# Attention in a two-layer decoder step: block transposes on VectorE and value products in 4 x 2 tiles

## The chip, the cores and the metric

One Trainium2 chip, one of its cores. The metric is the device time of one execution in microseconds; lower is better. The program is one launch that does two layers for 512 prompt tokens and 8 sample tokens together.

## The reference, cut to what matters

Each layer has one wide input projection, a depthwise conv branch, a sliding-window attention branch, two gates and an output projection. All arithmetic is in fp32.

```
h = rms_norm(x, norm_g)
glu, gate_a, q, k, v, gate_b, mg_a, mg_b = split(h @ w_in)
u = glu_a * sigmoid(glu_b)
c = conv31(u) + conv_b
c = silu(layer_norm(c)) * silu(gate_a)
y_a = c @ w_conv_out
o = attend(rope(q), rope(k), v, sinks)     # 16 heads of 64, 2 kv heads
y_b = (o * silu(gate_b)) @ w_attn_out
y = sigmoid(mg_a) * y_a + sigmoid(mg_b) * y_b
x = x + y @ w_out
```

The prompt's attention runs in 4 blocks of 128 queries. A block sees the 128 keys of the block before and its own 128, of these only the last 128 positions for each query, and one sink per head in the softmax's denominator:

```
s = (q @ k^T) / 8, masked to 0 <= diff < 128
m = max(max(s), sink);  p = exp(s - m)
o = (p / (sum(p) + exp(sink - m))) @ v
```

## The kernel before, in words

Activations lie with channels on the 128 partitions and 520 tokens (512 and 8) along the free dimension. A `Unit` is one 128-column slice of the weights against all 1024 input channels: its weights come in one DMA (`raw`), ScalarE rounds them to fp32r (`whi`, L109), VectorE takes the remainder (`wlo`, L110), and TensorE adds up, for each of 8 k-tiles and each half of 260 tokens, three products: hi x hi, lo x hi, hi x lo (L124). A half is 24 products, a unit 48. Two pairs of PSUM banks (`mmp`) hold units; four banks are left: two for scores and small sums (`psS`), one for transposed probabilities (`psT`), one for value products (`psV`).

The order of a layer: 16 units for the glu, then K, V, eight for Q (`W_Q`), eight for `gate_b` (`W_GB`, with Silu on the way out of PSUM, into `sgb`), then the attention loop, with eight units each of `W_MB` and `W_MA` (the merge gates) as filling between its steps, then eight of `W_GA`, eight of `W_YB` (on the attention's output `oh`/`ol`), eight of `W_YA` (on the conv's output `ch`/`cl`) and eight of `W_OUT`.

The attention loop has 32 steps, pairs (t, b) of a head pair t (one head of each kv head) and a block b. A step's `scores` makes the logits on TensorE (L474), masks them and takes the minimum on VectorE (L480), exponentiates and sums on ScalarE (L486) and scales the probabilities by the reciprocal (L489 to L491). Three steps later (`LAG`) `transposes` turns them on TensorE (L500) and ScalarE copies them to SBUF (L502). When the four blocks of t are turned, `values` multiplies them by v on TensorE (L509): the two kv heads write the lower and the upper 64 partitions of one bank. VectorE multiplies by the gate (L514, L517) and `split` rounds into `oh` and `ol` (L96, L97).

The conv is 31 taps per channel tile on VectorE: a multiply-add of 512 columns each, 240 a layer with the last ones (L563). They are traced with `tc.cur_priority` raised by 2000, so they are the work that VectorE does when nothing else is ready. Behind the last tap come the sums of the layer norm (L155, L160), mean (L574), subtraction (L577), squares (L187), `rstd`, scaling (L581), Silu (L602), the product with `sga` (L604) and the split into `ch` and `cl` (L96, L97), which `W_YA` needs.

A planner places the instructions at build time by priority and by its own prices; each engine then runs its list strictly in that order and waits on semaphores. DMAs for weights and q are issued from SP's queue, the small ones and those for the sample tokens from POOL's. A tile of a pool is given out again when its last reader is done.

Of the kernel before, what the change touches and what calls it, by code (L numbers as in the profile page):

```python
# [16 lines left out]
T = 512  # L17
NS = 8
TOK = T + NS
# [24 lines left out]
def hybrid_step(ctx, tc, x_in, w_in, par, const, rope, conv_st, kc_in, vc_in,  # L44
# [6 lines left out]
    gp = ctx.enter_context(tc.tile_pool(name="gp", bufs=42))  # L51
# [19 lines left out]
    def og(dt=F32):  # L71
        return gp.tile([128, TOK], dt, tag="o", bufs=16, name=name("o"))
# [21 lines left out]
    def split(src, n=TOK, new=g):  # L94
        hi, lo = new(F32R), new(F32R)
        A.copy(hi[:, :n], src)  # L96
        mark[0] = V.tensor_tensor(lo[:, :n], src, hi[:, :n].bitcast(F32), op=ALU.subtract)  # L97
        return hi, lo

    class Unit:  # L100


        def __init__(self, l, idx, hs, los, spare=False):
            self.hs, self.los = hs, los
            raw = wp.tile([128, KT, 128], F32, tag="raw", bufs=2, name=name("raw"))
            nc.sync.dma_start(raw, w_in[l, idx].rearrange("p (k c) -> p k c", k=KT))
            self.hi = wp.tile([128, KT, 128], F32R, tag="whi", name=name("whi"))
            self.lo = wp.tile([128, KT, 128], F32R, tag="wlo", name=name("wlo"))
            A.copy(self.hi, raw)  # L109
            V.tensor_tensor(self.lo, raw, self.hi.bitcast(F32), op=ALU.subtract)  # L110
            if spare:
                banks = [psT.tile([128, 512], F32, tag="T", name=name("T")),
                         psV.tile([128, 512], F32, tag="V", name=name("V"))]
                self.acc = [b[:, :HALF] for b in banks]
# [53 lines left out]
    def rstd(sums, halves=(0, 1)):  # L168
        y0, v, a = tmp("y0", 1), tmp("v", 1), tmp("a", 1)
# [53 lines left out]
    for l in range(L):  # L223
# [138 lines left out]
        A.copy(vb[:, :512], vtp)  # L362
        vsp = sbank()
# [37 lines left out]
        qs = {}  # L401

        def load_q(t):
            for kv in range(2):
                q = g(F32R)
                nc.sync.dma_start(q[:, :T].bitcast(F32), qscr[2 * t + kv])
                qs[t, kv] = q

        sgb = []
        for t in range(8):  # L410
            ps = Unit(l, W_GB + t, hh, hl).both()
            s = g()
            A.activation(two(s), ps, AF.Silu)  # L413
            sgb.append(s)
            if t == 3:
                load_q(0)
# [27 lines left out]
        def sample_transpose():  # L444
            pst = psT.tile([128, 512], F32, tag="T", name=name("pst"))
# [5 lines left out]
        def sample_values():  # L451
            pvs = psV.tile([128, 512], F32, tag="V", name=name("pvs"))
# [8 lines left out]
        oh, ol, mgb, mga = [], [], [], []  # L461
        pts, probs = {}, {}
        exp_ins = [None]

        def scores(t, b):
            if b == 0:
                if t < 7:
                    load_q(t + 1)
                pts[t] = ap.tile([128, 2, 7, 128], F32, tag="pts", bufs=1, name=name("pts"))
            k0, nk = (0, 128) if b == 0 else ((b - 1) * 128, 256)  # L470
            S3 = sbank().rearrange("p (v k) -> p v k", v=2)
            for kv in range(2):
                for j, K in enumerate((KH, KL)):
                    PE.matmul(S3[:, kv, :], qs[t, kv][:, b * 128:b * 128 + 128],  # L474
# [17 lines left out]
            probs[t, b] = p  # L492

        def transposes(t, b):
            p = probs.pop((t, b))
            PT = psT.tile([128, 2, 2, 128], F32, tag="T", name=name("PT"))
            nb = 1 if b == 0 else 2
            for kv in range(2):
                for kb in range(nb):
                    PE.transpose(PT[:, kv, kb, :], p[:, kv, kb * 128:kb * 128 + 128], ident)  # L500
            j0 = 2 * b + 1 - nb
            A.copy(pts[t][:, :, j0:j0 + nb, :], PT[:, :, :nb, :])  # L502

        def values(t):
            pv = psV.tile([128, 512], F32, tag="V", name=name("pv"))
            for j in (0, 2, 1, 3):
                nb = 2 if j < 3 else 1
                for kv in range(2):
                    PE.matmul(pv[kv * 64:kv * 64 + 64, j * 128:(j + nb) * 128],  # L509
                              vb[:, j * 128 + kv * 64:j * 128 + kv * 64 + 64],  # L510
                              pts[t][:, kv, 2 * j:2 * j + nb, :].rearrange("p a b -> p (a b)"),
                              start=(j == 0), stop=(j == 3))
            o = tmp("sq", 3)
            V.tensor_tensor(o[:, :T], pv, sgb[t][:, :T], op=ALU.mult)  # L514
            for kv in range(2):
                r = slice(kv * 64, kv * 64 + 64)
                V.tensor_tensor(o[r, T:], smp["o"][r, :, 2 * t + kv], sgb[t][r, T:], op=ALU.mult)  # L517
            a, b = split(o, new=og)
            oh.append(a)
            ol.append(b)  # L520

        LAG = 3
        order = [(t, b) for t in range(8) for b in range(4)]
        cur = None
        for n in range(len(order) + LAG + 1):
            if n < len(order):
                scores(*order[n])
                if n == 0:
                    sample_scores()
                if n % 2 == 0:  # L530
                    cur = Unit(l, (W_MB, W_MA)[n // 2 % 2] + n // 4, hh, hl)
                cur.half(n % 2)
                if n % 2 == 1:
                    m = g()
                    A.copy(two(m), cur.ps)
                    (mgb, mga)[n // 2 % 2].append(m)
# [4 lines left out]
            if n > LAG and order[n - LAG - 1][1] == 3:  # L541
                values(order[n - LAG - 1][0])
            if LAG <= n < len(order) + LAG:
                transposes(*order[n - LAG])
# [67 lines left out]
        yh, yl = [], []  # L612
        for i in range(KT):
# [3 lines left out]
            a, b = split(mga[i], new=og)  # L617
# [39 lines left out]
        def scale(hf):  # L657
            return rstd([sq.total(hf)], (hf,))
# [132 lines left out]
```

## Time and profile before

| | |
|---|---|
| Time, median of 3 runs | 1074.85 us (1074.48 to 1075.6) |
| The profiled execution's own time | 1074.0 us |
| Its span, first to last instruction | 1072.2 us |
| Mean granted TensorE clock | 0.997 |
| TensorE busy | 1053.9 us, 98% |
| VectorE busy | 854.2 us, 80% |
| ScalarE busy | 514.0 us, 48% |
| GpSimd busy | 79.3 us, 7% |
| Instructions | 21484 |

Busy time is the union of an engine's instructions; matmuls overlap in the array, so a busy TensorE isn't TensorE at its peak, and a matmul's duration is longer than the distance to the next. PE is TensorE, PEld its weight loads, DVE VectorE, ACT ScalarE, POOL GpSimd, SP the queue that issues most DMAs. A row names its line in the kernel, the tile written and the tiles read, without numbers.

### The profile page before, as it was taken

How to read it: one execution, taken by the hardware profiler on the slowest of the kernel's cores; microseconds unless marked ns; L12 is line 12 of the kernel's file. 1: busy time of each engine (PE TensorE's matmuls, PEld its weight loads, DVE VectorE, ACT ScalarE, POOL GpSimd, SP SyncE). 2: the span in 40 equal slices, each digit the busy share in tenths (PEclk: the TensorE clock that was granted, in tenths of full speed). 3: DMA queues.
4: the chain of work that ended last, by engine and by line, in shares of the span. 5: the costliest groups of instructions: out<-in, count | busy, mean ns of one | idle time of the engine just before them, and what ended most of it. 6: DMA issues, size and time to landing. Idle time of an engine off the chain costs nothing.

```text
span 1072.2 us, 21484 instructions
## 1 busy us (share of the span) xinstructions
PE 1053.9 (98%) x8724; PEld 1032.2 (96%) x8724; DVE 854.2 (80%) x1568; ACT 514.0 (48%) x949; POOL 79.3 (7%) x185
## 2 busy tenths in 40 slices
PE   7999999999999999999999999999999999999996
PEld 7999999999999999999999999999999999999995
DVE  5999999999999587455569999999999976944545
ACT  6622443356666785224453234334666686822321
POOL 1011221000001100000101013100000000000000
PEclk9999999999999999999999999999999999999998
DMA  5443574332222225223334337633232313252312
GB/s 218 130 129 111 168 253 149 101 117 80 99 82 72 68 70 189 95 99 113 134 99 139 119 119 247 201 103 119 80 116 67 95 41 99 86 175 96 98 60 80
DMA packets 44115, 126.41 MB, mean 118 GB/s; under 512 B 6176, under 2 KB 8816, under 8 KB 44016
## 3 DMA queue, kind: packets, MB, share of 16 engines
q1 hardware_dynamic: 37440, 110.23, 31.3%
q0 software_dynamic: 5136, 13.45, 3.9%
q8 instruction: 68, 1.11, 0.4%
q10 hardware_dynamic: 1440, 1.37, 0.4%
q14 instruction: 31, 0.25, 0.1%
HBM read 107.66 MB, written 17.36 MB: 117 GB/s over the span
## 4 chain that ended last, share of the span: by engine, by line
PE 95%; DVE 3%; DMA 1%; ACT 0%; issue 0%; SPq 0%; DVEq 0%; ACTq 0%
PE mm L124 85%; PE S L474 3%; PE pv L509 3%; PE PT L500 2%; DMA raw<-w 1%; PE T L124 1%; DVE g L663 1%; DVE wlo L110 1%; DVE sq L235 1%; PE S L160 0%; DVE g L97 0%; PE S L432 0%; PE pvs L454 0%; PE V L124 0%; ACT whi L109 0%
## 5 line engine op out<-in xcount | busy, mean ns | idle before, releaser
L124 PE MATMUL mm<-g,whi 128*128 128x260 f32 x4160 | 771.3, 284 | 7.6 <-ACT g L202 7.0
L124 PEld LDWEIGHTS mm<-g,whi 128*128 128x128 f32 x4160 | 646.3, 188 | 14.4 <-ACT g L202 7.4
L124 PE MATMUL mm<-g,wlo 128*128 128x260 f32 x2080 | 589.2, 284 | 0.0
L124 PEld LDWEIGHTS mm<-g,wlo 128*128 128x128 f32 x2080 | 393.1, 189 | 1.0 <-issue 0.8
L563 DVE SCALAR_TENSOR_TENSOR acc<-u,par,acc 128x512 f32<-128x512 f32 x464 | 329.6, 746 | 0.2
L109 ACT CAST whi<-raw 128x1024 fp32r<-128x1024 f32 x164 | 172.2, 1050 | 206.7 <-PE mm L124 167.3
L110 DVE TENSOR_TENSOR wlo<-raw,whi 128x1024 fp32r<-128x1024 f32 x164 | 200.4, 1223 | 55.3 <-ACT whi L109 55.1
L124 PE MATMUL mm<-o,whi 128*128 128x260 f32 x992 | 178.9, 282 | 0.4 <-DVE g L652 0.4
L124 PEld LDWEIGHTS mm<-o,whi 128*128 128x128 f32 x992 | 153.0, 188 | 0.6 <-DVE g L652 0.6
L124 PE MATMUL mm<-o,wlo 128*128 128x260 f32 x496 | 139.5, 282 | 0.0
L124 PEld LDWEIGHTS mm<-o,wlo 128*128 128x128 f32 x496 | 93.2, 188 | 0.0
L486 ACT ACTIVATE p<-p,sm 128x257 f32<-128x257 f32 (+1 forms) x128 | 60.9, 478 | 12.4 <-DVE sm L480 12.3
L502 ACT COPY pts<-PT 128x256 f32<-128x256 f32 (+1 forms) x64 | 33.8, 528 | 62.1 <-PE PT L500 61.9
L480 DVE CUSTOM_DVE_ANT_0 p<-S,con,nsk 128x256 f32<-128x256 f32 (+1 forms) x128 | 52.6, 448 | 10.9 <-PE PT L500 9.3
L478 POOL COPY p<-nsk 128x2 f32<-128x2 f32 x64 | 23.4, 369 | 360.8 <-PE PT L500 284.3
L615 DVE TENSOR_TENSOR g<-mm,g 128x520 f32<-128x520 f32 x16 | 11.2, 700 | 42.9 <-PE mm L124 42.9
L474 PE MATMUL S<-g,g 128*128 128x256 f32 x256 | 42.1, 284 | 0.0
L609 DVE TENSOR_TENSOR g<-mm,g 128x520 f32<-128x520 f32 x16 | 11.2, 699 | 32.0 <-PE mm L124 32.0
L413 ACT ACTIVATE g<-mm 128x520 f32<-128x520 f32 x16 | 9.7, 607 | 55.9 <-PE mm L124 55.9
L500 PE MATMUL PT<-con,p 128*128 128x128 f32 x224 | 35.6, 276 | 0.0
L474 PEld LDWEIGHTS S<-g,g 128*128 128x128 f32 x256 | 35.2, 189 | 0.4 <-DVE sm L480 0.4
L490 ACT ACTIVATE p<-p,sm 128x128 f32<-128x128 f32 (+1 forms) x64 | 29.8, 479 | 6.4 <-DVE sm L489 6.4
(167 smaller groups left out, 817.0 us busy)
## 6 DMA issues: line engine op xcount, KB each, us to landing
raw<-w SPq DMA_DIRECT2D x164, 512.0 KB, 3.4
qscr<-g SPq DMA_DIRECT2D x32, 256.0 KB, 4.5
g<-qscr SPq DMA_DIRECT2D x32, 256.0 KB, 3.7
g<-x SPq DMA_DIRECT2D x16, 260.0 KB, 7.2
g<-rope POOLq DMA_DIRECT2D x8, 260.0 KB, 4.0
xres<-g POOLq DMA_DIRECT2D x8, 260.0 KB, 2.3
g<-xres SPq DMA_DIRECT2D x8, 260.0 KB, 4.3
g<-conv_state POOLq DMA_DIRECT2D x8, 248.0 KB, 3.4
```

What stands on the lines that cost most here:

```text
L109: A.copy(self.hi, raw)
L110: V.tensor_tensor(self.lo, raw, self.hi.bitcast(F32), op=ALU.subtract)
L124: PE.matmul(self.acc[hf], a[:, k, :], b[k][:, c], start=(k == 0 and j == 0), stop=(k == KT - 1 and j == 2))
L474: PE.matmul(S3[:, kv, :], qs[t, kv][:, b * 128:b * 128 + 128], K[kv][:, k0:k0 + 256], start=(j == 0), stop=(j == 1))
L478: G.tensor_copy(p[:, :, nk:nk + 1], nsk[:, 2 * t:2 * t + 2].unsqueeze(2))
L480: V.tensor_tensor_reduce(out=p[:, kv, :nk], in0=S3[:, kv, :nk], in1=con[:, C_MASK + 256 - nk:C_MASK + 256], op0=ALU.add, op1=ALU.min, scal ...
L486: exp_ins[0] = A.activation(p[:, kv, :nk + 1], p[:, kv, :nk + 1], AF.Exp, bias=nm[:, kv:kv + 1], scale=-1.0, accum_out=dn[:, kv:kv + 1])
L490: A.mul(p[:, 0, :nk], p[:, 0, :nk], dn[:, 0:1])
L500: PE.transpose(PT[:, kv, kb, :], p[:, kv, kb * 128:kb * 128 + 128], ident)
L502: A.copy(pts[t][:, :, j0:j0 + nb, :], PT[:, :, :nb, :])
L509: PE.matmul(pv[kv * 64:kv * 64 + 64, j * 128:(j + nb) * 128], vb[:, j * 128 + kv * 64:j * 128 + kv * 64 + 64], pts[t][:, kv, 2 * j:2 * j + ...
L563: V.scalar_tensor_tensor(dst, us[i][:, k:k + T], cw(i, k), acc[i], op0=ALU.mult, op1=ALU.add)
```

## The change

The attention's steps are ordered by groups n of four head pairs and one block, (tg, b), with four steps t4 in each. The probabilities of a step are no longer transposed on TensorE through PSUM: VectorE transposes each 32 x 32 block in place of its own into `pts[n]`. Keys in those blocks stand rotated over the four groups of 32 partitions, so the values are kept in four copies, three of them rotated by 32, 64 and 96 partitions through DMAs from POOL's queue (`vr`). The value products have 32 rows and 64 columns each: for query group a and diagonal d, one product for each kv head, 128 columns wide (four head pairs of 32 queries), five diagonals added up in PSUM; the four query groups have a bank each. ScalarE copies the four banks, VectorE multiplies by the gates, and both split into wider tiles `oh` and `ol` of four head pairs. The separate pools `psT` and `psV` are gone; `psS` has four banks, for scores, values and all else. q is loaded for four heads and one block per DMA, rows of 512 bytes.

The units are reordered: four `W_GB` units stay ahead of the loop and four go into it, as its first filling, with their Silu after step 8; eight `W_MB` and four `W_MA` follow as filling, and four `W_MA` come behind the loop.

```diff
-    gp = ctx.enter_context(tc.tile_pool(name="gp", bufs=42))
+    gp = ctx.enter_context(tc.tile_pool(name="gp", bufs=41))
-    psS = ctx.enter_context(tc.tile_pool(name="psS", bufs=2, space=bass.MemoryType.PSUM))
-    psT = ctx.enter_context(tc.tile_pool(name="psT", bufs=1, space=bass.MemoryType.PSUM))
-    psV = ctx.enter_context(tc.tile_pool(name="psV", bufs=1, space=bass.MemoryType.PSUM))
+    psS = ctx.enter_context(tc.tile_pool(name="psS", bufs=4, space=bass.MemoryType.PSUM))
...
+        vr = ap.tile([128, 3, 512], F32, tag="vr", bufs=1, name=name("vr"))
+        for r in range(1, 4):
+            nc.gpsimd.dma_start(vr[:128 - 32 * r, r - 1, :], vb[32 * r:, :512])
+            nc.gpsimd.dma_start(vr[128 - 32 * r:, r - 1, :], vb[:32 * r, :512])
+        vrot = [vb[:, :512]] + [vr[:, r, :] for r in range(3)]
...
-                nc.sync.dma_start(q[:, :T].bitcast(F32), qscr[2 * t + kv])
+                nc.sync.dma_start(q3.bitcast(F32), qscr[h:h + 4, :, b * 128:b * 128 + 128]
+                                  .rearrange("h p c -> p h c"))
...
-            probs[t, b] = p
-
-        def transposes(t, b):
...
-            A.copy(pts[t][:, :, j0:j0 + nb, :], PT[:, :, :nb, :])
...
+            V.transpose(pts[n][:, t4, :, :nk], p[:, :, :nk])
+
+        def values(n):
+            tg, b = order[n]
+            pt4 = pts.pop(n)
+            pv = [sbank() for _ in range(4)]
+            for d in range(5):
+                for a in range(4):
+                    c = a + d if b else a + d - 4
+                    if c < 0:
+                        continue
+                    rows32 = slice(32 * a, 32 * a + 32)
+                    blk = c // 4 + (b - 1 if b else 0)
+                    for kv in range(2):
+                        col = blk * 128 + kv * 64
+                        PE.matmul(pv[a][kv * 64:kv * 64 + 64, :128],
+                                  vrot[d % 4][rows32, col:col + 64],
+                                  pt4[rows32, :, kv, 32 * c:32 * c + 32],
+                                  start=(c == 0 if b == 0 else d == 0), stop=(d == 4))
...
+            for a in range(4):
+                A.copy(o[:, :, 32 * a:32 * a + 32],
+                       pv[a][:, :128].rearrange("p (t q) -> p t q", t=4))
+            c = slice(b * 128, b * 128 + 128)
+            for t4 in range(4):
+                V.tensor_tensor(o[:, t4, :], o[:, t4, :], sgb[4 * tg + t4][:, c], op=ALU.mult)
+            gated(tg, c, o)
...
+        def gated(tg, c, o):
+            A.copy(oh[tg][:, :, c], o)
+            V.tensor_tensor(ol[tg][:, :, c], o, oh[tg][:, :, c].bitcast(F32), op=ALU.subtract)
...
+        fills = [(W_GB + t, sgb) for t in range(4, 8)]
+        fills += [(W_MB + i, mgb) for i in range(8)] + [(W_MA + i, mga) for i in range(4)]
         LAG = 3
...
+                if n == 8:
+                    prio = tc.cur_priority
+                    tc.cur_priority = prio - 300
+                    with tc.issue_after(exp_ins[0].ins):
+                        for t in range(4, 8):
+                            A.activation(sgb[t], sgb[t], AF.Silu)
+                        log_exp()
+                    tc.cur_priority = prio
...
+            if n >= LAG and (n - LAG) % 4 == 3:
+                values((n - LAG) // 4)
+        for i in range(4, 8):
+            merge_gate(i)
```

## Rows read from the trace of the kernel before

**Rows 1.** The page's part 1: busy us, share of the span, instructions.
```profile
PE 1053.9 (98%) x8724; PEld 1032.2 (96%) x8724; DVE 854.2 (80%) x1568; ACT 514.0 (48%) x949; POOL 79.3 (7%) x185
```

**Rows 2.** The page's part 2: busy tenths in 40 slices.
```profile
DVE  5999999999999587455569999999999976944545
...
PEclk9999999999999999999999999999999999999998
```

**Rows 3.** The chain of waits, whole run: shares of the span by engine and line.
```profile
PE 95%; DVE 3%; DMA 1%; ACT 0%; issue 0%; SPq 0%; DVEq 0%; ACTq 0%
...
by line: PE mm L124 84.6%; PE S L474 2.8%; PE pv L509 2.8%; PE PT L500 2.5%; DMA raw<-w 0.9%; PE T L124 0.8%; DVE g L663 0.6%; DVE wlo L110 0.6%; DVE sq L235 0.5%; PE S L160 0.4%; DVE g L97 0.4%; PE S L432 0.3%; PE pvs L454 0.3%; PE V L124 
```

**Rows 4.** TensorE's waits, whole run: total us, times, longest us.
```profile
PE mm L124 <- ACT g L202: 7.0, 1, 7.0
...
PE mm L124 <- DVE g L652: 0.4, 1, 0.4
```

**Rows 5.** The chain of waits, single pieces: start us, us, what.
```profile
267.46 0.44 PE PT L500 x4
...
273.51 0.58 PE pv L509 x4
...
280.10 1.23 PE pv L509 x12
...
356.76 0.88 PE S L160 x4
...
387.51 157.98 PE mm L124 x1323
```

**Rows 6.** Tile pv in a short window: us, busy (instructions) PE, PEld, DVE; clock, DMA.
```profile
262.91:263.15 0.24, 0.24 (x2) 0.19 (x4) 0.00 (x0) 1.00 0.55 222
```

**Rows 7.** VectorE's groups, 50 to 352 us: busy, mean ns | idle before, releaser.
```profile
L110 DVE TENSOR_TENSOR wlo<-raw,whi 128x1024 fp32r<-128x1024 f32 x44 | 53.8, 1222 | 7.3 <-ACT whi L109 7.3
L480 DVE CUSTOM_DVE_ANT_0 p<-S,con,nsk 128x256 f32<-128x256 f32 (+1 forms) x64 | 26.3, 449 | 5.5 <-PE PT L500 4.9 <-PE S L474 0.3
L491 DVE TENSOR_SCALAR p<-p,sm 128x256 f32<-128x256 f32 (+1 forms) x32 | 10.6, 335 | 0.0
...
L97 DVE TENSOR_TENSOR g<-sq,g 128x512 fp32r<-128x512 f32 (+1 forms) x8 | 5.3, 690 | 0.0
...
L292 DVE TENSOR_TENSOR sq<-g,par 128x248 f32<-128x248 f32 x7 | 2.9, 414 | 0.0
...
L517 DVE TENSOR_TENSOR sq<-g,g 64x8 f32<-64x8 f32 x16 | 2.5, 158 | 0.1
```

**Rows 8.** Busy time by stretch: us, PE, PEld, DVE, ACT, POOL; clock, DMA.
```profile
49.00:353.00 304.00, 303.47 (x2528) 295.27 (x2528) 287.04 (x585) 145.13 (x311) 32.27 (x71) 1.00 0.38 123
353.00:417.00 64.00, 64.00 (x530) 62.57 (x529) 48.73 (x69) 50.01 (x77) 4.72 (x11) 1.00 0.28 91
```

**Rows 9.** VectorE's timeline, 345 to 420 us: start, us, instruction [idle before, releaser].
```profile
351.47 0.74 DVE L563 SCALAR_TENSOR_TENSOR u<-u,par,acc 128x512 f32<-128x512 f32 x1
...
358.30 0.70 DVE L97 TENSOR_TENSOR o<-sq,o 128x520 fp32r<-128x520 f32 x1 [5.35 <-ACT o L96]
...
372.83 1.23 DVE L110 TENSOR_TENSOR wlo<-raw,whi 128x1024 fp32r<-128x1024 f32 x1 [3.33 <-ACT whi L109]
...
416.39 0.70 DVE L97 TENSOR_TENSOR g<-sq,g 128x520 fp32r<-128x520 f32 x1
```

**Rows 10.** TensorE's timeline: the first product on the conv's output, layer 0.
```profile
442.11 0.28 PE L124 MATMUL mm<-g,whi 128*128 128x260 f32 x1
```

**Rows 11.** ScalarE's groups, 208 to 375 us.
```profile
L502 ACT COPY pts<-PT 128x512 f32<-128x512 f32 (+1 forms) x32 | 16.9, 528 | 31.7 <-PE PT L500 31.7
...
L183 ACT ACT_TABLE_LOAD x1 | 1.3, 1283 | 0.0
...
L457 ACT COPY g<-pvs 128x128 f32<-128x128 f32 x1 | 0.3, 266 | 0.2 <-PE pvs L454 0.2
```

**Rows 12.** The page's part 6: DMA issues, KB each, median us to landing.
```profile
g<-qscr SPq DMA_DIRECT2D x32, 256.0 KB, 3.7
```

More of the change, by code (lines that the diff above doesn't have):

```diff
@@ L92, in hybrid_step, with split @@
     V.memset(eps, EPS)
-    def split(src, n=TOK, new=g):
-        hi, lo = new(F32R), new(F32R)
+    def split(src, n=TOK, out=None):
+        hi, lo = out or (g(F32R), g(F32R))
         A.copy(hi[:, :n], src)
@@ L458, in sample_values, with scores @@
             smp["o"] = osam[:, :128].rearrange("p (n h) -> p n h", n=NS)
-        oh, ol, mgb, mga = [], [], [], []
-        pts, probs = {}, {}
+        mgb, mga = [], []
+        pts = {}
         exp_ins = [None]
[L465 to L469, printed above, removed]
+        def scores(n, t4):
+            tg, b = order[n]
+            t = 4 * tg + t4
+            if t4 == 0:
+                load_q(n + 1)
+                pts[n] = ap.tile([128, 4, 2, 256], F32, tag="pts", bufs=1, name=name("pts"))
             k0, nk = (0, 128) if b == 0 else ((b - 1) * 128, 256)
@@ L504, in values @@
[L504 to L520, printed above, removed]
+            V.transpose(pts[n][:, t4, :, :nk], p[:, :, :nk])
@@ new lines, in values @@
+        def values(n):
+            tg, b = order[n]
+            pt4 = pts.pop(n)
[13 more added lines that the diff above has]
+                                  start=(c == 0 if b == 0 else d == 0), stop=(d == 4))
+            if b == 0:
+                oh.append(og(F32R))
+                ol.append(og(F32R))
+            o = tmp("sq", 3)[:, :512].rearrange("p (t q) -> p t q", t=4)
+            for a in range(4):
[5 more added lines that the diff above has]
+            gated(tg, c, o)
+            if b == 3:
+                os = small(32).rearrange("p (t n) -> p t n", t=4)
+                for t4 in range(4):
+                    t = 4 * tg + t4
+                    for kv in range(2):
+                        r = slice(kv * 64, kv * 64 + 64)
+                        V.tensor_tensor(os[r, t4, :], smp["o"][r, :, 2 * t + kv], sgb[t][r, T:],
+                                        op=ALU.mult)
+                gated(tg, slice(T, TOK), os)
@@ L522, in hybrid_step, with merge_gate @@
+        def gated(tg, c, o):
+            A.copy(oh[tg][:, :, c], o)
+            V.tensor_tensor(ol[tg][:, :, c], o, oh[tg][:, :, c].bitcast(F32), op=ALU.subtract)
+        def merge_gate(i):
+            m = g()
+            A.copy(two(m), Unit(l, W_MA + i, hh, hl).both())
+            mga.append(m)
+        fills = [(W_GB + t, sgb) for t in range(4, 8)]
+        fills += [(W_MB + i, mgb) for i in range(8)] + [(W_MA + i, mga) for i in range(4)]
         LAG = 3
-        order = [(t, b) for t in range(8) for b in range(4)]
+        steps = 4 * len(order)
@@ L524, in hybrid_step @@
         cur = None
-        for n in range(len(order) + LAG + 1):
-            if n < len(order):
-                scores(*order[n])
+        for n in range(steps + LAG):
+            if n < steps:
+                scores(n // 4, n % 4)
                 if n == 0:
                     sample_scores()
+                w, out = fills[n // 2]
                 if n % 2 == 0:
-                    cur = Unit(l, (W_MB, W_MA)[n // 2 % 2] + n // 4, hh, hl)
+                    cur = Unit(l, w, hh, hl)
                 cur.half(n % 2)
@@ L540, in hybrid_step @@
                 sample_values()
[L541 to L544, printed above, removed]
+            if n >= LAG and (n - LAG) % 4 == 3:
+                values((n - LAG) // 4)
+        for i in range(4, 8):
+            merge_gate(i)
+        oh = [oh[t // 4][:, t % 4, :] for t in range(8)]
+        ol = [ol[t // 4][:, t % 4, :] for t in range(8)]
         def cw(i, k):
@@ L616, in hybrid_step @@
             V.tensor_tensor(mga[i], mga[i], mgb[i], op=ALU.add)
-            a, b = split(mga[i], new=og)
+            if i % 4 == 0:
+                yg = [og(F32R), og(F32R)]
+            a, b = split(mga[i], out=[t[:, i % 4, :] for t in yg])
             yh.append(a)
```

54 lines of the change are left out of this document (25 added, 29 removed).

## The prediction

> **What bounds the kernel now.** I read the engine totals first, then the slices, then the chain of waits, then the stretches around the conv. The totals show TensorE busy 1053.9 of 1072.2 us, and VectorE second with 854.2 [rows 1]. The slices show that VectorE's 80% is no even load: it is at nine tenths or more up to slice 12 and again from slice 21 to 32, and near half between and after [rows 2]. The granted clock is at its upper level throughout. The chain runs on TensorE for 95% of the span [rows 3], and TensorE's waits are four rows, from 7.0 us at the very start down to 0.4 [rows 4]. So what leaves TensorE's list shortens the kernel, until another engine is late.
>
> The second step is to see how late VectorE may be. In layer 0 the last conv tap starts at 351.47, and the last low half of the gated conv (`ch`/`cl`, L97) at 416.39, done at 417.1 [rows 9]. TensorE takes its first `W_YA` product, which needs all of `ch`, at 442.11 [rows 10]. So there is a margin of 25 us, which I take for both layers, and behind it VectorE, filled with conv taps to 287.0 of 304 us [rows 8], is the next bound.
>
> **What leaves TensorE.** By the chain the transposes of the probabilities (L500) hold 2.5% and the value products (L509) 2.8% of 1072.2: 26.8 + 30.0 = 56.8 us [rows 3]. By pieces: a transpose group of four takes 0.44, a values call 0.58 + 1.23 [rows 5]; 48 of the former and 16 smaller ones at half give 24.6, 16 calls give 29.0, together 53.6. I take 56.8; a miss of 3 us is inside what follows.
>
> **What comes to TensorE.** The trace doesn't have 32-row tiles. What it has is two-column tiling: the two `kv` halves of L509 write PSUM partitions 0 to 63 and 64 to 127. An fp32 product stands as two passes, and in a window of 0.24 us two passes are in flight with nothing else [rows 6]. Twelve passes, eight of 256 columns and four of 128, end in 1.23 us [rows 5]. A 260-column fp32 pass of the sums takes 0.88/4 = 0.22 us [rows 5], so one behind the other the twelve would take 8 x 0.217 + 4 x 0.108 = 2.17. In pairs it is 1.08, and the other 0.15 us is entry and exit of the piece. So passes on different tiles do run side by side, and a pass of 128 columns holds its tile 0.108 us.
>
> A new call has five diagonals `d`, each 4 rows x 2 columns = 8 products, 16 passes; block 0 has 10 row products in place of 20. If all eight tiles run side by side, a diagonal costs 2 x 0.108 = 0.217 us: 5 x 0.217 + 0.15 = 1.24 a call, 4 x 0.217 + 0.15 = 1.02 for block 0. A layer has 6 and 2: 9.5 us, two layers 19.0. This is my lower bound. The upper bound is that only the column pair overlaps: 20 pairs x 0.217 + 0.15 = 4.49, block 0 2.32, a layer 31.6, two layers 63.2. I take 19.0, because the only tiles in the trace that could overlap did, without loss, and the change gives every row group a PSUM bank of its own. TensorE's list then shrinks by 56.8 - 19.0 = 37.8 us, 18.9 a layer.
>
> The Trainium skill, page TensorE: Matmul & The Clock Gate, section Part 3, says that tiles in different row groups overlap too, with starts some 4 ns apart; no row here shows it, and by it the sum stays as it is. The same page (Part 1, on the 56 ns gap) speaks against the change: starts never come closer than about 25 ns however short the matmul. By that the 1120 passes would take about 28 us plus the entries, 30 in place of 19, an estimate from the page; the two passes of a window above don't test it, since they are only two. As VectorE is late anyway (next part), it would give about 1054.
>
> **What comes to VectorE.** In each layer 24 transposes of 512 columns and 8 of 256. The trace has none. The nearest rows are two-input operations SBUF to SBUF: 512 columns in 0.69, 248 in 0.41; back to back, starts stand about 0.08 closer than durations. 24 x 0.61 + 8 x 0.33 = 17.3 us. Lower bound, the scaling of 256 columns at 0.335 whatever the width: 32 x 0.335 = 10.7. Upper bound, half the rate, as the 1024-column row at 1.22: 24 x 1.22 + 8 x 0.69 = 34.8 [rows 7]. I take 17, as an operation that moves each element once is nearest to the first rows. The gating was 8 x (0.69 + 0.69) + 16 x 0.158 = 13.6; now it is 32 products of 128 columns at 0.25 (between the rows of 8 and 248 columns), 8 subtractions of 512 at 0.69, and 18 small ones: 8.0 + 5.5 + 2.8 = 16.3, so +3 [rows 7]. VectorE gets 20 us a layer, all ahead of the conv's end, because the conv taps have the lowest priority.
>
> **What hides, and what would be late.** The loads of q keep their number and bytes, in rows of 512 bytes; each landed in 3.7 us before [rows 12] and is asked for one group, four steps, ahead, some 15 us. The six DMAs for the rotated values go into POOL's queue ahead of the `vscr` and `vc` transfers, while the `W_Q` units run; the sample values that need those come behind six `W_Q` and four `W_GB` units of 5.7 us. ScalarE loses 32 copies of 0.528 and gets 32 of 0.27, and two table loads of 1.28: about 6 us less [rows 11]. The new wait is for banks: a values call takes all four score banks, and the next scores wait for the four copies on ScalarE, about 1 us. A half unit of 24 products at 157.98/1323 = 0.119, 2.9 us (a whole unit 5.7) [rows 5], covers that; without cover it would be 16 x 1 us. `pts` has one buffer, so the next group's first transpose waits for the values; queued behind it on VectorE are the mask operations of newer steps, weight splits and taps, and TensorE's next scores wait for those. The three steps of lag cover it. Moving four `W_GB` units into the loop and four `W_MA` units behind it changes no engine's sum; it starts attention 4 x 5.7 = 23 us sooner.
>
> **The sum.** Where TensorE alone counts, `W_YA` could begin at 442.1 - 18.9 = 423.2. VectorE's last `ch` was at 417.1. Add 20 for the new work and the splits and evacuations of the 25/5.7 = 4.4 units that TensorE has yet to pass before `W_YA`: 4.4 x (1.14 + 0.62) = 7.7, durations of 1.22 and 0.70 less 0.08, together 444.8. Of VectorE's idle time, 17 us up to 353 and 15 us up to 417 [rows 8], I let go what hung on transposes: 4.9 waiting for L500 inside the loop [rows 7], 3.3 at 372.8 and some 5 at 358.3, when ScalarE's queue stood behind late transposes [rows 9]. That gives 431.6, so TensorE waits 8.4 us a layer. 37.8 - 16.8 = 21.0. The profiled execution took 1074.0, its span 1072.2 and 1.8 around it; 1074.0 - 21.0 = 1053.0, and against the median of 1074.85, 0.85 higher, 1054.
>
> With the bounds of the transposes: at 10.7 us the wait is 2 us, 1041; at 34.8 it is 26 a layer and more than the 18.9 saved, 1089. Measurements of this kernel differ by 0.1%, so I call 0.2% no change.
>
> **Rivals.**
> (a) VectorE hides its new work: the order closes more of the 32 us of idle than I let it. Then TensorE's whole saving stands: 1037. For it: VectorE waits 7.3 us for weight casts in this stretch [rows 7], which other taps could fill. Against: those waits are from an order fixed ahead.
> (b) The change doesn't do what it says, row tiles don't overlap: 63.2 - 56.8 = 6.4 more on TensorE. `W_YA` could begin at 445.3, VectorE is done at 431.6, no wait: 1081. For it: no row shows row tiles. Against: column tiles, as independent, overlap fully.
> (c) Slower, by the order laid out ahead. The engines' order is fixed by a planner at build time, and its price for small products isn't in the trace. If it prices the passes one after another, a call is 70 x 0.108 = 7.6 us in the plan, 6.3 more than on the chip; over 8 calls it puts 50 us of conv taps a layer between the attention's VectorE steps. On the chip TensorE then waits there for VectorE. It decides at 18.9 us a layer of such waits; half of the 50 gives +6 a layer, 1087, all of it 1138. Against: inside the loop now VectorE waits for TensorE's transposes (4.9 us), TensorE never for VectorE [rows 4, 7], so the planner's TensorE is, if anything, too quick. For it: the present pairs are few.
>
> **Chances.** Forecast (1041 to 1068) 0.50; (a) 0.13; (b) 0.12; (c) 0.20; a wait that just eats the gain 0.05. Faster: 0.50 + 0.13 and a little of the last, 0.65; same 0.07; slower 0.28. The range from 1036 to 1090 leaves out the best end of (a) and the worse half of (c). The likeliest case alone is 1041 to 1068.
>
> **What would show it.** TensorE: values pieces of about 1.1 us with eight passes in flight, not 4 us. VectorE: transposes of about 0.65 us; last tap near 385; in the chain, VectorE or ScalarE pieces of some 8 us a layer ahead of the first `W_YA` product. (a) has no such piece; (b) has values pieces over 4 us; (c) has TensorE waiting inside the loop for the transposes or the mask operations. I am wrong if a transpose takes over 1.1 us, or banks or `pts` make TensorE wait 1 us a call.

## The result, and the profile after

The change makes the kernel slower: 1101.54 us (1100.18 to 1103.12, 4 runs) against 1074.66, ratio 1.0247, 95% interval 1.0234 to 1.026. The forecast was 1054 (range 1036 to 1090) and faster. The span of the profiled execution is 1101.2 us, 29.0 more than before.

The page's parts 1, 2 and 4 of the changed kernel (compare [rows 1 to 3]): busy us and share; busy tenths in 40 slices; shares of the chain by engine.

```profile
PE 1043.3 (95%) x9364; PEld 1028.8 (93%) x9364; DVE 888.0 (81%) x1684; ACT 512.7 (47%) x969; POOL 78.5 (7%) x197
...
DVE  5999989999999568355569999999999966844545
...
PEclk9999999998899899999999999999989989999998
...
PE 69%; DVE 24%; ACT 4%; issue 3%; DMA 1%; SPq 0%; DVEq 0%; ACTq 0%
```

TensorE's list did become shorter, but the chain, 95% on TensorE before, runs for 24% on VectorE, and the granted clock falls in several slices of the loop. TensorE's waits in layer 0, from 170 to 545 us, where before had next to none [rows 4]:

```profile
PE mm L120 <- ACT g L569: 8.4, 2, 5.9
PE mm L120 <- ACT g L550: 3.0, 1, 3.0
PE S L519 <- DVE pts L504: 2.9, 3, 1.2
PE S L486 <- ACT sq L528: 2.0, 3, 1.0
PE mm L120 <- ACT g L631: 1.1, 1, 1.1
```

With two smaller rows they make 18.4 us; the same reading of layer 1 (700 to 1090) gives 20.8 before the final norm. "ACT g L569" is the copy of a finished gate unit. What it waits for is seen in the chain of waits around the longest of these, 5.9 us (start us, us, what):

```profile
290.10 1.31 DVE acc L606 x2
291.42 0.20 DVE p L503
291.62 5.30 DVE acc L606 x8
296.91 0.07 DVE pts L504
296.98 0.21 issue
297.20 0.14 DVE pts L504
297.34 0.19 issue
297.52 0.40 DVE pts L504
297.92 0.18 DVE sq L532
298.10 0.02 issue
298.13 0.60 ACT g L569
298.73 0.04 issue
298.77 4.27 PE mm L120 x21
```

A value call ended at 288.69. The next group's transposes (L504) then stand in VectorE's list behind a run of taps (L606), the gate product behind them, and ScalarE's copy behind that, as its target was the gate just read. TensorE takes up its units at 298.77. From the end of a call to the next transposes it is 1.1 to 8.1 us in layer 0, with 0 to 11 taps started in between: 7.2 us with seven, 8.1 with eleven, 1.1 with one. The last scaling that these transposes need (L503) is done at 291.62 in the chain above; eight taps run before them all the same.

Busy time of PE, PEld, DVE, ACT and POOL by stretch, then granted clock and DMA (compare [rows 8]; the first three stretches are those at the lower level in layer 0, the last the attention loop):

```profile
261.15:271.39 10.24, 9.21 (x109) 8.17 (x108) 10.24 (x26) 6.75 (x19) 0.19 (x1) 0.50 0.20 61
295.28:302.11 6.83, 3.34 (x15) 3.34 (x16) 6.83 (x18) 2.58 (x7) 0.67 (x3) 0.50 0.27 79
360.13:366.96 6.83, 5.71 (x26) 5.71 (x27) 1.89 (x7) 6.80 (x14) 0.00 (x0) 0.50 0.00 0
...
180.00:353.00 173.00, 160.03 (x1622) 155.87 (x1629) 170.96 (x426) 92.86 (x241) 7.15 (x28) 0.95 0.28 87
```

VectorE is full in the loop, 170.96 of 173 us, and TensorE is not. Of the 39.2 us of waits, 12.9 and 14.0 come up to the last tap of their layer (354.2 and 890.5 us). The largest of the others, 5.3 us at 903.34 in layer 1, isn't due to taps: VectorE itself sits idle for 8.1 us there, as the scaling that its last transpose needs (L502) stands behind thirteen sigmoids of the merge gates in ScalarE's list:

```profile
907.79 0.71 DVE L504 STREAM_TRANSPOSE pts<-p 128x512 f32<-128x512 f32 x1 [8.11 <-ACT p L502]
```

In layer 0 the clock stands at 0.50, 1.2 GHz, for 6.8 to 10.2 us at each of TensorE's three waits of over 2.5 us: behind the first, and from within the other two. Over the run the mean is 0.973 against 0.997: 1101.2 x 0.027 - 1072.2 x 0.003 = 26.5 us at full speed that weren't granted.

The sum closes to a few us. 56.8 us left TensorE. The value calls that nothing disturbs take 1.36 us, in block 0 1.02, from first start to the next unit: 12 x 1.36 + 4 x 1.02 = 20.4, and 20.4 - 56.8 = -36.4. So -36.4 + 18.4 + 20.8 + 26.5 = +29.3, beside 29.0 measured. Some 4 us of it count twice, where the clock is low during a wait.

### The profile page after: what moved, and what is told of

It reads as the page before. It is cut to its first block, busy times and chain, and to the rows that moved or that the text cites. A ratio compares the mean times of both kernels' runs of the same rounds, so it can differ in the third digit from the quotient of the medians.

```text
span 1101.2 us, 22904 instructions
## 1 busy us (share of the span) xinstructions
PE 1043.3 (95%) x9364; PEld 1028.8 (93%) x9364; DVE 888.0 (81%) x1684; ACT 512.7 (47%) x969; POOL 78.5 (7%) x197
## 3 DMA queue, kind: packets, MB, share of 16 engines
q1 hardware_dynamic: 49728, 110.23, 30.7%
## 4 chain that ended last, share of the span: by engine, by line
PE 69%; DVE 24%; ACT 4%; issue 3%; DMA 1%; SPq 0%; DVEq 0%; ACTq 0%
PE mm L120 65%; DVE acc L606 10%; DVE wlo L108 3%; DVE p L492 3%; DVE pts L504 2%; PE S L120 2%; DVE p L503 1%; DVE sq L532 1%; PE S L486 1%; DMA raw<-w 1%; DVE g L709 1%; DVE o L546 1%; ACT L637 0%; ACT L169 0%; DVE u L624 0%
## 5 line engine op out<-in xcount | busy, mean ns | idle before, releaser
L120 PEld LDWEIGHTS mm<-g,whi 128*128 128x128 f32 x4160 | 654.5, 192 | 34.1 <-ACT g L569 15.0
L120 PEld LDWEIGHTS mm<-g,wlo 128*128 128x128 f32 x2080 | 398.2, 191 | 1.3 <-issue 1.0
L606 DVE SCALAR_TENSOR_TENSOR acc<-u,par,acc 128x512 f32<-128x512 f32 x464 | 327.8, 742 | 0.1
L504 DVE STREAM_TRANSPOSE pts<-p 128x512 f32<-128x512 f32 (+1 forms) x64 | 37.9, 622 | 10.5 <-ACT p L502 10.5
L490 POOL COPY p<-nsk 128x2 f32<-128x2 f32 x64 | 16.4, 260 | 373.4 <-DVE pts L504 368.5
L502 ACT ACTIVATE p<-p,sm 128x256 f32<-128x256 f32 (+1 forms) x64 | 30.4, 476 | 23.5 <-DVE sm L501 23.0
L486 PE MATMUL S<-g,g 128*128 128x256 f32 x256 | 36.7, 291 | 4.4 <-ACT sq L528 4.4
L652 DVE TENSOR_TENSOR g<-mm,g 128x520 f32<-128x520 f32 x16 | 11.1, 695 | 27.8 <-PE mm L120 27.8
L545 ACT CAST o<-sq 128x512 fp32r<-128x512 f32 x16 | 10.0, 622 | 50.2 <-DVE sq L532 50.1
L519 PE MATMUL S<-pts,g 32*64 32x128 f32 x448 | 21.5, 323 | 12.0 <-DVE pts L504 10.6
```

What stands on the lines that cost most here:

```text
L120: PE.matmul(self.acc[hf], a[:, k, :], b[k][:, c], start=(k == 0 and j == 0), stop=(k == KT - 1 and j == 2))
L486: PE.matmul(S3[:, kv, :], qs[n, 2 * t4 + kv], K[kv][:, k0:k0 + 256], start=(j == 0), stop=(j == 1))
L490: G.tensor_copy(p[:, :, nk:nk + 1], nsk[:, 2 * t:2 * t + 2].unsqueeze(2))
L502: A.mul(p[:, 0, :nk], p[:, 0, :nk], dn[:, 0:1])
L504: V.transpose(pts[n][:, t4, :, :nk], p[:, :, :nk])
L519: PE.matmul(pv[a][kv * 64:kv * 64 + 64, :128], vrot[d % 4][rows32, col:col + 64], pt4[rows32, :, kv, 32 * c:32 * c + 32], start=(c == 0 if ...
```

## The experiments

Two theories stood at the start. P: the fixed order takes the value products for longer than they are, puts conv taps into that time on VectorE, and TensorE waits. Q: the change's own couplings do it, four banks held by a values call and one buffer `pts`. "Inside the loop" is from a layer's first transpose to the end of its last value call; TensorE waits 16.9 and 19.7 us there in the changed kernel, in layers 0 and 1. Ratios are to the kernel before, with 95% intervals. Median times of before were 1075.0 in e1 to e4, 1075.4 in e5 to e8, 1074.7 in e9 to e12, 1075.2 in e13 to e15 and 1074.8 in e16 to e18.

**e1, one diagonal of five.**
```diff
-            for d in range(5):
+            for d in (4,):
...
-                                  start=(c == 0 if b == 0 else d == 0), stop=(d == 4))
+                                  start=True, stop=True)
```


> Leaves out four of the five diagonals of the value products (8 products a call in place of 40 or 20); all else is the changed kernel. On TensorE that removes at most 16 x 0.9 = 14 us. Theory P (the planner prices the small products one behind another, so it puts conv taps into gaps that the chip doesn't have): TensorE's waits in the loop, 18 to 21 us a layer, and the low clock behind them, 12 to 14 us a layer, mostly go: 1030 to 1055. Theory Q (four banks and the one buffer of pts make the steps wait on the chip whatever the plan): the waits stay, 1085 to 1092.

1066.88 us, ratio 0.9923 (0.9906 to 0.9939): 34.7 us less, where the products left out were worth at most 16 (0.8 x 20.4). The order is laid out anew, and now 0 to 4 taps start between a call and the next transposes. The waits inside the loop fall to 9.6 and 9.3 us, by about half, where P had them mostly go: it speaks for P, but the time came out above P's range, with 5.1 us of TensorE's waits for transposes left in each layer.

**e2, the last pair's taps behind the last transpose.**
```diff
-        with tc.issue_after(ready):
-            for i0 in range(0, KT, 2):
+        for i0 in range(0, KT, 2):
+            with tc.issue_after(turned[0].ins if i0 == 6 else ready):
```


> The taps of the last two channel tiles (60 of 240 a layer, 40 us of VectorE) may only come behind the last transpose; nothing is left out. If taps ahead of the attention's steps are what TensorE waits for, the loop's waits fall below 8 us a layer, the last tap moves from 354 to 375-390, and the first W_YA product waits for the conv by some 10 us: 1050 to 1080. If the waits come from banks and pts alone, they stay, and the later conv adds to them: 1105 to 1130.

1091.85, ratio 1.0155 (1.014 to 1.017). This lies between the two ranges. The early calls, which still had taps at hand, kept up to 8 behind them; the late calls had none, and their transposes came 0.4 to 2.3 us after. The last value call ended at 337.5, in the changed kernel at 376.9. The waits inside the loop are 11.4 and 9.9 us, not below 8: the longest in layer 0, 5.2 us, comes late, when no tap is left there, and ScalarE runs sigmoids during it.

**e3, sigmoids behind the last scaling on ScalarE.**
```diff
+            mul_ins[0] = A.mul(p[:, 0, :nk], p[:, 0, :nk], dn[:, 0:1])
...
-            with tc.issue_after(exp_ins[0].ins):
+            with tc.issue_after(mul_ins[0].ins):
```


> The sigmoids of the merge gates come behind the last scaling of probabilities on ScalarE's queue in place of behind the last exponential; nothing is left out. The last transpose of a layer waited 8.1 us for that scaling, and the last values, the layer norm's totals and W_YA are behind it. If this tail is on the path: 1082 to 1092. If W_YA is late for other reasons: 1098 to 1104.

1108.44, ratio 1.0309 (1.0294 to 1.0325): slower, and above both ranges. The last values came 8 us sooner, and their copies then stood behind the sigmoids: TensorE waits 3.8 and 5.6 us for them, new in this run.

**e4, the gates in their old order.**
```diff
-        for t in range(4):
+        for t in range(8):
...
-        fills = [(W_GB + t, sgb) for t in range(4, 8)]
-        fills += [(W_MB + i, mgb) for i in range(8)] + [(W_MA + i, mga) for i in range(4)]
+        fills = [(w + i, out) for i in range(8) for w, out in ((W_MB, mgb), (W_MA, mga))]
```


> The changed kernel with the gates in the old order: eight W_GB units ahead of the loop, eight W_MB and eight W_MA inside it, no Silu inside. If the move of the gates (attention 23 us sooner, fewer taps done before it) is what hurts: 1070 to 1085. If it is the new transposes and value products, and their order, whatever the gates: 1095 to 1110.

1113.14, ratio 1.0355 (1.034 to 1.0371), above its second range. The reordering isn't what costs; it helps by 12 us here.

**e5 to e7, the taps dosed.** In e5 the taps of the last four of the eight channel tiles are held back: seven may come only behind the third transpose of each group, the rest behind the last transpose of all; e6 has five in place of seven; e7 is e5 with the cut of e1.
```diff
+        def behind(i0, j):
+            if i0 < 4:
+                return ready
+            k = (j + 60 * (i0 - 4) // 2) // 7
+            return turns[4 * k + 2] if k < 8 else turns[-1]
...
+                    with tc.issue_after(behind(i0, j)):
+                        V.scalar_tensor_tensor(dst, us[i][:, k:k + T], cw(i, k), acc[i],
```


> Nothing is left out. From the third pair of channel tiles on, seven conv taps may come only behind the third transpose of a group of four steps, the rest behind the last transpose, so none is at hand for the gap that the fixed order sees between the value products and the next group's transposes. Theory P (the order fixed ahead prices the value products far above what they take, fills that time with taps on VectorE, and TensorE then waits, at a lower granted clock): TensorE's waits inside the attention loop fall from some 19 us a layer to under 8 and the half-clock stretches with them, and the conv chain is next: 1045 to 1062 us. Rival Q (the four banks and the one buffer of transposed probabilities couple the engines whatever the order): the waits stay above 12 us a layer with no taps in them, and the time at 1085 or more.

> As e5, with five taps behind the third transpose of a group in place of seven, so more of them are left behind the last transpose. Theory P: the loop is as free of waits as in e5, and the conv chain ends some 16 taps x 0.7 us = 11 us later a layer if VectorE has room for them in the loop: 1055 to 1080 us, above e5. Rival Q: as e5 or slower, 1085 or more, with the same waits.

> As e5, and only one of the five diagonals of the value products is computed, so four fifths of them are left out (the output is not the reference's). Theory P: with no taps at hand the overpriced products have little left to cost, so against e5 it gains only what the chip takes for them, 0.8 x 19 = 15 us at most, less where VectorE decides: 1040 to 1060 us, 0 to 15 below e5 (the same cut without the pacing took 34.7 us off). Rival Q: it gains 25 us or more on e5, as the banks are held for less time.

e5: 1078.98, ratio 1.0047 (1.0031 to 1.0063), 22.6 us below the changed kernel with the same work. No tap stands between a call and the next transposes, and the waits inside the loop fall to 5.6 and 8.9 us, but the time is above P's range. e6: 1091.76, 1.0155 (1.014 to 1.017). By its time it falls to Q, by its waits it doesn't: 5.0 and 7.0 us are left inside the loop, and the last tap starts at 394.7, in e5 at 386.5. e7: 1089.06, 1.0127 (1.0112 to 1.0143), 10 us above e5 though it does less: the sign was not as expected. e7's waits of TensorE, 170 to 545 us, and busy time by stretch, the loop and a part of what follows it:

```profile
PE mm L120 <- ACT g L94: 19.9, 2, 19.3
PE S L156 <- DVE ssum L151: 8.0, 1, 8.0
PE mm L120 <- ACT g L640: 0.5, 1, 0.5
```
```profile
180.00:340.00 160.00, 160.00 (x1420) 157.83 (x1419) 138.34 (x381) 106.26 (x272) 12.85 (x31) 1.00 0.31 100
...
419.67:450.39 30.72, 5.77 (x21) 4.84 (x22) 23.07 (x37) 22.90 (x32) 0.74 (x6) 0.50 0.15 52
```

In the loop TensorE doesn't wait at all, busy 160.00 of 160. But the last tap starts at 405.6, later than in e5, for a reason that isn't shown, and TensorE waits 28 us for the conv's sums and `ch`, with 30.7 us at half clock. So with the taps held back the conv's end is the next bound, as the prediction had it, and the question became how many taps the loop can carry.

**e8, the gates reordered in the kernel before, nothing else.**
```diff
-        for t in range(8):
+        for t in range(4):
...
+        fills = [(W_GB + t, sgb) for t in range(4, 8)]
+        fills += [(W_MB + i, mgb) for i in range(8)] + [(W_MA + i, mga) for i in range(4)]
...
-                    cur = Unit(l, (W_MB, W_MA)[n // 2 % 2] + n // 4, hh, hl)
+                    cur = Unit(l, fills[n // 2][0], hh, hl)
```


> The kernel before with the gates' projections in the new order alone (four first gates ahead of the loop, four in it; four W_MA units behind it), with the old transposes and the old value products. By the prediction's step it changes no engine's sum: 1070 to 1079 us. If starting attention earlier helps VectorE: TensorE was never waiting there, so still the same. If the new order costs waits of its own (the late SiLU pass and its table loads on ScalarE): 1080 to 1095 us, and this part would carry some of the 27 us lost.

1074.03, ratio 0.999 (0.9981 to 1.0): no change, as expected.

**e9 and e10, more taps.** e9 is e5 with nine taps and the sigmoids behind the last `W_MA` copy; e10 is e9 with two urgent taps behind each of a group's transposes in place of the nine.
```diff
-            k = (j + 60 * (i0 - 4) // 2) // 7
+            k = (j + 60 * (i0 - 4) // 2) // 9
...
+            copy_ins[0] = A.copy(two(m), Unit(l, W_MA + i, hh, hl).both())
...
-            with tc.issue_after(exp_ins[0].ins):
+            with tc.issue_after(copy_ins[0].ins):
```


> Nothing is left out. e5 with nine taps behind each third transpose in place of seven, and the sigmoids of the merge gates only behind the copy of the last W_MA gate. In e5 VectorE had some 1.6 us idle per group of four steps, room for two taps. Theory P: 16 taps x 0.74 = 12 us of the conv leave the stretch behind the loop in each layer at no cost to the loop, and TensorE's wait of 5.2 us for a W_MA copy behind the sigmoids goes: 1058 to 1074 us, below the kernel before. If VectorE has no such room in the loop, each further tap is a wait of TensorE: 1079 to 1095.

> Nothing is left out. As e9, with two taps behind each of the four transposes of a group, at the priority of the loop's own work, eight a group. Theory P: what counts is that no run of taps stands ahead of the late transposes, so the loop's waits stay as small as in e5 or become smaller, and 8 taps x 0.74 = 6 us a layer leave the stretch behind the loop: 1062 to 1078 us. If it's the taps of the steps themselves that delay the masks and so the scores: 1079 to 1095, with TensorE waiting for mask operations.

e9: 1064.65 us (4 runs), ratio 0.9907 (0.9892 to 0.9922): faster than both kernels, with all of the work done. The page's part 2 and the stretch of the loop in e9:

```profile
PEclk9999999999999999999999999999999999999998
```
```profile
180.00:353.00 173.00, 168.54 (x1855) 164.53 (x1854) 165.85 (x427) 110.81 (x282) 9.33 (x32) 1.00 0.27 90
```

In the same 173 us TensorE does 1855 matmuls where the changed kernel did 1622, at full clock, and the last value call ends at 336.7 in place of 376.9. Its waits in this layer are 10.9 us, of which 8.4 come behind the loop. The four banks are held as before, and TensorE's waits for their copies ("ACT sq") are 1.5 us in layer 0, in the changed kernel 2.0, so this part of Q is small. e10: 1080.18, 1.0048 (1.0033 to 1.0063), with TensorE waiting for mask operations (3.8 us of "DVE sm L493" in layer 0), which fits its second case: taps at the loop's own priority stand ahead of the steps' small operations.

**e11 and e12, two buffers for the transposed probabilities, and the control.** Both use unrotated values in every tile, so the products' values differ; e12 has one buffer.
```diff
-                pts[n] = ap.tile([128, 4, 2, 256], F32, tag="pts", bufs=1, name=name("pts"))
+                pts[n] = ap.tile([128, 4, 2, 256], F32, tag="pts", bufs=2, name=name("pts"))
```


> Two buffers for the transposed probabilities, so that the next group's transposes wait for no value product; to make room the rotated copies of the values are left out (every tile takes its values from the unrotated ones, so the products' values differ, not their number or shape). The taps are as free as in the changed kernel. Theory P: the order still sees value products that last too long, and puts all taps into the loop; VectorE is full there and TensorE waits: 1085 to 1103 us. Rival Q (the one buffer couples the engines): the waits for transposes vanish, 1045 to 1065.

> The control of e11: one buffer as in the changed kernel, with the rotated copies left out likewise. Both theories: as the changed kernel, 1095 to 1106 us, and what e11 differs from it is the second buffer alone.

e11: 1126.3, ratio 1.0478 (1.0461 to 1.0496). e12: 1116.22, 1.0388 (1.0373 to 1.0404). Both are above what was expected. The second buffer doesn't help, so this part of Q falls. In layer 0 of e11 at most 3 taps start between a call and the transposes that come next, in e12 up to 9; yet TensorE waits as long as in e12 for the call's own last transposes. First e11, then e12, TensorE's waits, 170 to 545 us:

```profile
PE S L515 <- DVE pts L500: 19.2, 5, 9.0
```
```profile
PE S L515 <- DVE pts L500: 18.9, 5, 6.7
```

So P had to be mended: it isn't the gap behind a call alone that costs. In e11 as in the changed kernel 117 taps of layer 0 stand between the first and the last transpose, and VectorE is full; the stretch from 240 to 360 us in e11:

```profile
240.00:360.00 120.00, 103.10 (x1117) 98.34 (x1116) 119.01 (x292) 60.35 (x172) 10.32 (x24) 0.89 0.19 66
```

e12 is 15 us above the changed kernel, though it only leaves out six DMAs and one tile of a pool. Another order is the likely reason, which isn't shown further; differences of this size between two orders need not come from what the edit is about.

**e13 to e15, sigmoids, taps, and eleven.** e13 is e5 with e9's sigmoids alone, e14 with nine taps alone, e15 is e9 with `// 11`.

> Nothing is left out. e5 with the sigmoids only behind the copy of the last W_MA gate, seven taps as in e5. If the sigmoids' place only removes the wait of TensorE for a W_MA copy (0.7 us in layer 0, 5.2 in layer 1, with some 3 us at half clock behind it): 1070 to 1076 us. If the conv's end decides behind the loop: as e5, 1077 to 1081.

> Nothing is left out. e5 with nine taps a group, the sigmoids where the change has them. If the conv's end decides behind the loop: 16 x 0.74 = 12 us a layer sooner, of which TensorE can use what its own list leaves, 1064 to 1072 us. If it's TensorE's waits on ScalarE that count: as e5, 1076 to 1081.

> Nothing is left out. e9 with eleven taps a group. If VectorE still has room in the loop: some 10 us a layer of taps leave the stretch behind it and TensorE's waits for the gated conv's products there (8.4 us in layer 0, 5.9 in layer 1 of e9) go: 1052 to 1062. If the loop is full, 16 taps x 0.74 = 12 us a layer fall on the masks and transposes, and TensorE's waits of 1 us and more come back: 1068 to 1090.

e13: 1074.33, ratio 0.9991 (0.9982 to 1.0). e14: 1071.83, 0.997 (0.996 to 0.9979). Both came out as their first case. e14 changes nothing but the place of the taps and is 29.7 us below the changed kernel, so this alone takes away its whole loss. The sigmoids are worth 4.7 us on e5, two more taps a group 7.2, both 14.3. e15: 1076.07, 1.0015 (1.0005 to 1.0025), but for another reason than either case named. TensorE waits 8.8 us for "ACT g L640", and ScalarE's list had sigmoids ahead of the last softmax steps. Its timeline there in e15:

```profile
344.63 0.62 ACT L643 ACTIVATE g<-g 128x520 f32<-128x520 f32 x1
345.15 0.62 ACT L644 ACTIVATE g<-g 128x520 f32<-128x520 f32 x1
345.79 1.28 ACT L499 ACT_TABLE_LOAD   x1
347.08 0.51 ACT L499 ACTIVATE p<-p,sm 128x257 f32<-128x257 f32 x1
347.50 0.19 ACT L499 ACTIVATION_READ_ACCUMULATOR p<-p,sm 128x1 f32 x1
347.70 1.28 ACT L643 ACT_TABLE_LOAD   x1
```

**e16 to e18, all sigmoids behind the attention's last rounding, nine, eleven and thirteen taps.**
```diff
+            ins = A.copy(oh[tg][:, :, c], o).ins
+            if c.start < T:
+                copy_ins[0] = ins
...
+            with tc.issue_after(copy_ins[0]):
```


> Nothing is left out. e9 with all sigmoids of the merge gates behind the attention's last rounding into oh, so that none stands ahead of a softmax step. If ScalarE's order in the last steps costs nothing in e9: as e9, 1062 to 1067 us. If the sigmoids in one block now hold up the copies of the W_GA units: 1067 to 1073.

> Nothing is left out. e16 with eleven taps a group. If e15 lost its time to ScalarE's order alone: 1055 to 1063 us, below e9 and e16, and TensorE waits for nothing of VectorE inside the loop. If the loop is full for VectorE with nine: 1066 to 1080, with waits for masks or transposes.

> Nothing is left out. e16 with thirteen taps a group. By busy time VectorE has some 7 us idle of 160 in e9's loop, or one tap a group, so thirteen must be too many under theory P: 1068 to 1090 us, above e17, with waits for transposes or masks as in the changed kernel. If the number of taps in the loop doesn't matter: as e17.

e16: 1078.93, ratio 1.0037 (1.0024 to 1.0051). e17: 1080.8, 1.0059 (1.0043 to 1.0076). e18: 1096.95, 1.0206 (1.019 to 1.0221). All three are above their ranges. In e16 and e17 the sixteen sigmoids in one block hold up the copies of the `W_GA` units, 7.7 and 7.0 us in layer 0, 11.1 and 10.2 in layer 1. Inside the loop they tell what they were for. Busy time from 180 to 340 us in e16, e17 and e18, and e18's waits for transposes:

```profile
180.00:340.00 160.00, 157.33 (x1764) 153.52 (x1763) 152.84 (x406) 97.40 (x260) 9.39 (x32) 1.00 0.29 94
```
```profile
180.00:340.00 160.00, 158.67 (x1709) 154.96 (x1709) 154.89 (x407) 96.61 (x255) 9.17 (x31) 1.00 0.29 94
```
```profile
180.00:340.00 160.00, 151.88 (x1639) 148.06 (x1638) 156.15 (x407) 93.84 (x248) 9.24 (x31) 0.99 0.28 91
```
```profile
PE S L520 <- DVE pts L505: 2.7, 2, 2.2
```

With thirteen taps TensorE gets through fewer matmuls in the same time and waits for transposes again. With eleven it waits for none, but the attention's last transpose stands at 343.0, with nine at 333.3. So the room ends between eleven and thirteen; whether eleven cost the kernel anything, 1.9 us between e16 and e17, isn't clear beside what another order alone can do.

Nor is it the number of taps alone. e4 has 92 taps between the first and the last transpose of layer 0, e17 88. In e4 all of them start by 339.4, with nothing to hold them back, and TensorE waits 17.5 us up to there; in e17 they come in doses behind third transposes, and it waits 1.1 us in the whole loop. (The two differ in the gates and the sigmoids, too.) First e4's longest rows of waits, 170 to 545 us, then those of e17 that lie inside the loop:

```profile
PE S L519 <- DVE pts L504: 11.2, 4, 4.3
PE mm L120 <- ACT g L568: 6.3, 3, 4.7
PE S L486 <- ACT sq L528: 5.9, 3, 3.5
```
```profile
PE S L487 <- ACT sq L529: 0.8, 2, 0.5
PE S L520 <- DVE sm L493: 0.3, 1, 0.3
```

## Why the prediction was wrong

**What leaves TensorE.** Right: the transposes and old products are gone, and the chain has no piece of them.

**What comes to TensorE.** Right within 8%. I took 1.24 and 1.02 us a call and 19.0 us in all; measured 1.36 and 1.02, 20.4. A call of block 0 in the changed kernel, TensorE's timeline, with its first products and the unit behind them:

```profile
311.69 0.54 PE L519 MATMUL S<-pts,vr 32*64 32x128 f32 x14
...
311.97 0.27 PE L519 MATMUL S<-pts,vr 32*64 32x128 f32 x1
...
312.30 0.48 PE L519 MATMUL S<-pts,g 32*64 32x128 f32 x6
312.71 0.39 PE L120 MATMUL mm<-g,wlo 128*128 128x260 f32 x1
```

40 passes in 1.02 us, each lasting some 0.27: tiles in different rows and columns do run side by side. So rival (b) falls. The Trainium skill, page TensorE: Matmul & The Clock Gate (Part 1, the 56 ns gap), says that starts never come closer than about 25 ns; here 80 passes on eight tiles follow within 1.36 us, 17 ns apart in the mean, and the measurement decides.

**What comes to VectorE.** Right. The transposes, in the page's part 5 of the changed kernel:

```profile
L504 DVE STREAM_TRANSPOSE pts<-p 128x512 f32<-128x512 f32 (+1 forms) x64 | 37.9, 622 | 10.5 <-ACT p L502 10.5
```

0.70 us for 512 columns by itself, 37.9 / 2 = 19.0 us a layer, against 17.3 taken. VectorE's busy time grew by 888.0 - 854.2 = 33.8 us, 16.9 a layer, where 20 were forecast. The last `ch` was split at 434.0, 431.6 was forecast.

**What hides, and what would be late: here it failed.** Two sentences were wrong. "The three steps of lag cover it" was said of `pts` and of the masks, splits and taps behind which a transpose stands; and the sum took the conv taps as work that gives way, so that VectorE's extra 20 us would show at the last tap, "near 385", while TensorE went on. But a low priority acts when the order is laid out, not on the chip. The order put all taps that were left into the loop, the last done at 354.2, hardly later than before [rows 9], and the 20 us fell on the attention: its last value call ended at 376.9, where e14, with the same work and only the taps held back, ends it at 345.9, and e9, with the sigmoids moved as well, at 336.7. TensorE, which had become the quicker of the two in the loop, waited 18.4 and 20.8 us. It didn't wait for `ch`, where the forecast had its 8.4 us a layer: `W_YA` began at 455.4, 21 us after `ch`.

**Rival (c)** is what happened, by its time (1087 to 1138) and by its sign (TensorE waiting inside the loop), at a chance of 0.20. My argument against it, that TensorE never waited for VectorE before [rows 4, 7], says nothing of an order that is laid out anew with other work in it. Its boundary, 18.9 us of waits a layer, was just passed (39.2 in both); by the waits alone the change would have come out near even: -36.4 + 39.2 = +2.8, some 1077. Why the order puts so many taps there is shown only in part: with a fifth of the products it puts fewer (e1: 106 between the first and the last transpose of layer 0, in place of 117), which fits a price that is too high, but the price itself stands in no trace.

**The term that was missing** is TensorE's clock. I read it at its upper level throughout [rows 2] and priced a wait at its own length. In the changed kernel each wait of over 2.5 us has 3.4 to 10.2 us at half clock behind it or from within it: 26.5 us in all, about as much as the whole loss.

**Rival (a)**, 1037, and the forecast's 1054 were not reached by any order that was tried. e9 has 1064.65, with 18.6 us of waits on TensorE left in both layers (10.9, and 7.7 before the final norm); whether an order without them exists wasn't found.

## What to carry to other kernels

When work moves from the engine that bounds a stretch to one that is nearly full there, compare the two in that stretch alone: VectorE went from 287 of 304 us to 171 of 173, and TensorE's saving turned into waits. Low-priority filling in an order fixed ahead doesn't give way on the chip; hold it back with explicit dependencies and find the dose by trial (with e9's sigmoids, seven, nine and eleven taps a group gave 1074, 1065 and 1076 us, the last with an order on ScalarE that cost it 8.8 us). Look at the other engines' lists too: the sigmoids of ScalarE held up steps in several of these runs. And price a wait of TensorE with the slow stretch behind it, not by its length.

## What the runs showed of the hardware

The granted clock fell to 0.50 (1.2 GHz) behind short waits: in the changed kernel behind one of 2.55 us (258.04 to 260.59), for 10.24 us; in e7, with waits of 8.0 and 19.3 us, it stood there from 419.67 to 450.39. In the kernel before, whose TensorE hardly waits between its start and its last sums, the only such stretch begins at 1066.2, at the very end.

Fp32 passes of 128 columns on eight 32 x 64 tiles start 17 ns apart in the mean and each last some 0.27 us; a VectorE transpose of 512 fp32 columns in 32 x 32 blocks takes 0.70 us, as long as a plain two-input operation of that width [rows 7].
